# Transposes of the second query tile and one low value product given out first in each attention group

## The chip, the cores and the metric

The kernel runs on one core of one Trainium2 chip. The metric is the device time of one execution in microseconds (us); lower is better. A core has five engines, each with its own in-order instruction queue: PE (matrix products, its weight loads shown apart as PEld), DVE (vector), ACT (scalar functions, copies), POOL (vector work without access to PSUM) and SP, which here issues most of the memory transfers. PSUM is the accumulator memory that PE writes; DVE and ACT read it.

## The reference

One decoder layer on 2048 tokens of width 1024, in float32. The part that matters here is attention: 8 "forgetting" heads (softmax with a cumulative forget bias) and 8 "stick-breaking" heads, each of width 64, causal, then a product with the values.

```python
def one_block(args):                                  # forgetting heads, a block of 128 queries
    s = jnp.einsum('bhqd,bhkd->bhqk', q_blk, k) * scale
    s = s + F_blk[..., None] - F[:, :, None, :]
    s = jnp.where(causal, s, -jnp.inf)
    p = jax.nn.softmax(s, axis=-1)
    return jnp.einsum('bhqk,bhkd->bhqd', p, v)

def one_block(args):                                  # stick-breaking heads
    z = jnp.einsum('bhqd,bhkd->bhqk', q_blk, k) * scale
    log_one_minus_beta = jnp.where(strict, jax.nn.log_sigmoid(-z), 0.0)
    rest = lax.cumsum(log_one_minus_beta, axis=3, reverse=True) - log_one_minus_beta
    a = jnp.where(strict, jnp.exp(jax.nn.log_sigmoid(z) + rest), 0.0)
    return jnp.einsum('bhqk,bhkd->bhqd', a, v)
```

Around it stand a modulated RMS norm, one input projection (queries, keys, values, forget logits), a per-head norm, an output projection with a gated residual, and a gated MLP with a width-3 convolution. All of that is the same before and after.

## The kernel before, in words

The program runs in stages. First come the conditioning vector and the first 512 tokens' projections. Then come 32 attention units (stick-breaking heads first, then forgetting heads; four head pairs of each kind, and four blocks of 512 tokens for each pair). While a unit's attention runs, the projections of later units are issued between its pieces as filler: `L342` (queries and keys) and `L413` (values), whose inputs `hp` SP loads from memory at L468. Behind the last unit the output projection (L912), the MLP up (L1315) and the MLP down (L1614, L1609) follow.

Precision is kept by splitting each float32 operand into a high part, rounded to the faster type, and a low part, the rest. A product then needs several passes: high by high, high by low, low by high.

Inside a unit two query tiles of 128 rows are handled together (`qi` 0 and 1, the first and the second tile). For each tile `logits` (L596 and L597) puts a chunk of up to 512 logits into a PSUM bank `ps_qk` (two of them). For stick-breaking heads ACT makes two sigmoids `r` and `a` (L630, L631), POOL masks the diagonal (L633), and a DVE scan (L636) turns `a` into weights; `a` and `r` have seven buffers each. For forgetting heads DVE adds the bias and finds the row's extreme (L675), and ACT takes the exponential (L679) over the whole row.

Then `weighted` is called for each attention group, a pair of key blocks of 128 and two query tiles; there are 576 groups. It

- transposes up to four 128x128 blocks of weights on PE into one PSUM bank `ps_pt` (L606; three such banks): first those of the first query tile for key blocks 1 and 0, then those of the second tile for key blocks 0 and 1. In a group on the diagonal the first of the four is left out,
- copies the bank on ACT into the high half of the tile `at` (L610) and lets DVE subtract that copy from the bank into the low half (L611). `at` has three buffers,
- adds four products to the unit's accumulator `ps_pv` (L615): key block 0 by the high half, key block 0 by the low half, and the same for key block 1.

The order of instructions on each engine isn't the order of the code. A planner replays the program against its own model of times when the program is built, and puts into each engine's queue whatever is ready there first; ties go by the order of the code. So the two transposes of the first tile may be queued as soon as that tile's scan is done in the model, other work may come between them and the second tile's, and the high product may stand ahead of its low one with other work between. `tc.issue_after(x)` tells the planner that the instructions inside the block are to be queued behind `x` on the same engine. Each engine then runs its queue in order, and waits at an instruction whose inputs are not there.

When a head is done, ACT and DVE empty the accumulator (L737, L738). `ps_pv` has one buffer, so the next head's first product waits for that. At the end of a unit SP stores the result `oT` (L740), and SP's queue too is in order, so loads of `hp` behind that store wait with it.

## Time and profile before

| | |
|---|---|
| median of 3 runs | 2949.18 us (2945.81 to 2950.16) |
| the profiled execution: span from its first to its last instruction | 2941.4 us |
| busy share of PE / PEld / DVE / ACT / POOL | 97% / 84% / 74% / 57% / 31% |
| from 60 to 1440 us (attention with projections): PE busy | 1334.3 of 1380 us |
| in the same stretch: transposes L606, value products L615 | 2045 and 2158 PE instructions |

The page of the profile gives for its execution the span alone, no separate time with what lies around it. The span is 7.8 us (0.26%) under the median of the runs.

How to read it: a row of the timeline joins equal instructions that follow each other ("x4"), with the start of the first and the time from there to the end of the last. PE's instructions overlap: the next one starts long before the row's last one has ended, so what an instruction costs is the distance from one start to the next, not its duration. Ends on PE are modelled. "Idle before" is time in which the engine had nothing running before an instruction, with what ended it. The view of one line adds up such idle time on PE and on PEld for the same instruction, the view of waits gives the two apart.

### The profile page before, as it was taken

What the parts mean: (1) busy time and instruction counts of PE and PEld (TensorE: products, weight loads), DVE (VectorE), ACT (ScalarE), POOL (GpSimd) and SP (SyncE); (2) the same over time, 40 slices, a digit from 0 to 9 for tenths busy, and PEclk for the clock granted to TensorE, in tenths of its full rate; (3) what the DMA queues carried; (4) which work ended last, traced back from release to release, by engine and by line L of the source; (5) the groups of instructions that cost most, each with busy time, mean ns of one, the idle gap of its engine ahead of it and who ended that gap; (6) DMA issues with size and microseconds to landing.
All of it is one profiled execution on the core that took longest, in us unless ns stands there. A gap on an engine that the chain in (4) does not pass through costs nothing.

```text
span 2941.4 us, 45922 instructions
## 1 busy us (share of the span) xinstructions
PE 2867.8 (97%) x15772; PEld 2459.7 (84%) x15772; DVE 2179.5 (74%) x3464; ACT 1686.0 (57%) x3187; POOL 901.1 (31%) x967
## 2 busy tenths in 40 slices
PE   8999999999999999999999999999999999999998
PEld 7888888888988988888888788888788888888887
DVE  5787778877886656658843788888998888575476
ACT  5776767677776656658744554444444445433342
POOL 0431322243032423231213344444254543142200
PEclk8999999999999999999999999999999999999999
DMA  9749756867469794794537775554754444975644
GB/s 293 255 139 321 236 188 207 301 211 229 162 212 356 269 277 139 232 323 140 182 120 233 245 232 128 130 136 129 236 132 125 130 130 132 309 257 185 216 158 151
DMA packets 348346, 601.89 MB, mean 205 GB/s; under 512 B 34672, under 2 KB 178800, under 8 KB 348112
## 3 DMA queue, kind: packets, MB, share of 16 engines
q1 hardware_dynamic: 324208, 558.06, 57.7%
q0 software_dynamic: 10880, 20.97, 4.3%
q10 hardware_dynamic: 13024, 19.93, 1.9%
q8 instruction: 124, 2.03, 0.3%
q14 instruction: 110, 0.90, 0.1%
HBM read 420.77 MB, written 177.02 MB: 203 GB/s over the span
## 4 chain that ended last, share of the span: by engine, by line
PE 46%; DMA 3%; DVE 2%; SPq 1%; ACT 1%; issue 1%; POOL 0%; DVEq 0%; ACTq 0%; POOLq 0%
PE ps_o L1315 19%; PE ps_t L1315 7%; PE ps_o L1614 6%; PE ps_t L1614 3%; PE ps_bc L1614 3%; PE ps_o L912 1%; PE ps_pv L615 1%; DMA r<-rstd 1%; PE ps_bc L912 1%; PE ps_pt L606 1%; PE ps_o L1609 1%; DMA wo<-wos 1%; DMA hm<-hf_m 1%; SPq L895 1%; DVE op L46 1%
## 5 line engine op out<-in xcount | busy, mean ns | idle before, releaser
L1315 PE MATMUL ps_o<-op,wu 128*128 128x512 f32 x2592 | 608.0, 389 | 2.0 <-DVE snap L1366 1.5
L1315 PEld LDWEIGHTS ps_o<-op,wu 128*128 128x128 f32 x2592 | 486.2, 188 | 103.9 <-DVE snap L1366 1.9
L611 DVE TENSOR_TENSOR at<-ps_pt,at 128x512 fp32r<-128x512 f32 (+1 forms) x576 | 366.1, 652 | 100.2 <-ACT at L610 97.3
L636 DVE TENSOR_TENSOR_SCAN a<-r,a 128x512 f32<-128x512 f32 (+2 forms) x320 | 368.3, 1167 | 77.8 <-ACT a L631 39.9
L342 PE MATMUL ps_pj<-hp,w_qk 128*128 128x512 f32 x1512 | 411.2, 403 | 14.5 <-DMA hp<-hs 12.9
L610 ACT ACTIVATE at<-ps_pt 128x512 fp32r<-128x512 f32 (+1 forms) x576 | 318.5, 576 | 139.1 <-PE ps_pt L606 123.1
L615 PE MATMUL ps_pv<-at,V 128*128 128x256 f32 x2216 | 386.8, 292 | 9.3 <-DVE at L611 4.2
L615 PEld LDWEIGHTS ps_pv<-at,V 128*128 128x128 f32 x2216 | 320.9, 190 | 39.8 <-DVE at L611 11.4
L342 PEld LDWEIGHTS ps_pj<-hp,w_qk 128*128 128x128 f32 x1512 | 275.4, 190 | 71.0 <-DMA hp<-hs 16.2
L45 ACT ACTIVATE wu<-wuraw 128x512 fp32r<-128x512 f32 x204 | 128.9, 632 | 248.5 <-PE ps_o L1315 190.1
L596 PE MATMUL ps_qk<-K,Q 128*128 128x512 f32 (+2 forms) x640 | 265.7, 416 | 5.6 <-ACT a L631 3.3
L413 PE MATMUL ps_pj<-w_v,hp 128*128 128x256 f32 (+1 forms) x1536 | 236.6, 288 | 2.1 <-DVE hp L422 1.6
L597 PE MATMUL ps_qk<-K,Q 128*128 128x512 f32 (+2 forms) x640 | 235.7, 369 | 0.0
L1315 PE MATMUL ps_t<-op,wu 128*128 128x512 f32 x888 | 220.8, 390 | 1.0 <-DVE op L46 1.0
L413 PEld LDWEIGHTS ps_pj<-w_v,hp 128*128 128x128 f32 x1536 | 209.0, 189 | 10.9 <-DVE q L373 1.5
L630 ACT ACTIVATE r<-ps_qk 128x512 f32<-128x512 f32 (+2 forms) x320 | 173.1, 541 | 58.2 <-PE ps_qk L597 55.5
L46 DVE TENSOR_TENSOR wu<-wuraw,wu 128x512 fp32r<-128x512 f32 x204 | 189.6, 930 | 18.1 <-ACT wu L45 16.7
L1315 PEld LDWEIGHTS ps_t<-op,wu 128*128 128x128 f32 x888 | 166.4, 188 | 36.5 <-DVE op L46 1.8
L606 PE MATMUL ps_pt<-edge,a 128*128 128x128 f32 x1088 | 185.1, 274 | 8.4 <-DVE a L636 7.8
L1614 PE MATMUL ps_o<-op 128*128 128x512 f32 x840 | 191.5, 389 | 0.0
L1614 PEld LDWEIGHTS ps_o<-op 128*128 128x128 f32 x840 | 157.7, 188 | 32.7
L679 ACT ACTIVATE p<-p,mn 128x128 f32<-128x128 f32 (+15 forms) x128 | 153.9, 1203 | 53.3 <-DVE mn L675 52.2
(342 smaller groups left out, 5237.6 us busy)
## 6 DMA issues: line engine op xcount, KB each, us to landing
hp<-hs SPq DMA_DIRECT2D x224, 512.0 KB
wuraw<-in_w_up_dram SPq DMA_DIRECT2D x80, 512.0 KB
ra<-g SPq DMA_DIRECT2D x136, 256.0 KB
rb<-in_w_down_dram SPq DMA_DIRECT2D x108, 256.0 KB
g<-u SPq DMA_DIRECT2D x80, 256.0 KB
hs<-hp SPq DMA_DIRECT2D x32, 512.0 KB
hp<-in_w_ada_dram SPq DMA_DIRECT2D x32, 512.0 KB
qk_fox<-q SPq DMA_DIRECT2D x32, 512.0 KB
```

The source lines that it names most:

```text
L46: (lo_engine or nc.gpsimd).tensor_sub(lo, src, f(hi))
L342: nc.tensor.matmul(acc, w[kt][:, a, n], h[:, bb], start=kt == 0 and i == 0, stop=kt == KT - 1 and i == 2)
L413: nc.tensor.matmul(av[:, t * width:(t + 1) * width], hts[kt][:, a, tok], w[1][kt][:, bb, 0:width], start=kt == 0 and m == 0, stop=kt == KT ...
L596: nc.tensor.matmul(b[:, :cw], Q[:, hl, 0, qcols], K[:, hl, :cw], start=True, stop=False)
L597: marks.append(nc.tensor.matmul(b[:, :cw], Q[:, hl, 1, qcols], K[:, hl, :cw], start=False, stop=True).ins)
L606: nc.tensor.transpose(b[:, i * P:(i + 1) * P], blk(kts[kk], qi), ident)
L610: copies = [nc.scalar.activation(at[:, 0, lo:], b[:, lo:], AF.Copy).ins, nc.vector.tensor_sub(at[:, 1, lo:], b[:, lo:], f(at[:, 0, lo:])).ins]
L611: nc.vector.tensor_sub(at[:, 1, lo:], b[:, lo:], f(at[:, 0, lo:])).ins]
L615: m = nc.tensor.matmul(o[:, 0:2 * P], V[kt // 4][:, kt % 4, hl, :], rhs, start=first and kk == 0 and w == 0, stop=last and kk == 1 and w == 1)
L636: nc.vector.tensor_tensor_scan(rev, r[:, 0:need][:, ::-1], rev, 0.0 if right[qi] is None else right[qi][:, 0:1], ALU.mult, ALU.add)
L1315: nc.tensor.matmul(b, w[:, p, j], o[:, q], start=first and i == 0, stop=last and i == 2, skip_group_check=True)
L1614: nc.tensor.matmul(b, a[:, p, t * P:(t + 1) * P], w[:, q], start=first and i == 0, stop=last and i == 2, skip_group_check=True)
```

## The change

Inside `weighted` the order of the transposes in the code is turned round: second tile, key block 1, then second tile, key block 0, then the first tile's two. The first one given out becomes `lead`, and the other three are to be queued behind it. Of the products the low one of each key block now stands ahead of the high one, and the first high product is to be queued behind the first low one. The same instructions run on the same data; the accumulator's start and stop flags move with the order.

```diff
         order = [(1, 0), (0, 0), (0, 1), (1, 1)]
-        for i, (kk, qi) in enumerate(order):
+        lead = None
+        for i in (3, 2, 1, 0):
+            kk, qi = order[i]
             if not (diag and i == 0):
-                nc.tensor.transpose(b[:, i * P:(i + 1) * P], blk(kts[kk], qi), ident)
+                with tc.issue_after(lead) if lead else nullcontext():
+                    m = nc.tensor.transpose(b[:, i * P:(i + 1) * P], blk(kts[kk], qi), ident).ins
+                lead = lead or m
...
         for kk, kt in enumerate(kts):
-            for w in range(2):
+            for w in (1, 0):
                 rhs = at[:, w].rearrange("p (s q) -> p s q", q=P)[:, 0:4:3, :] if kk else at[:, w, P:3 * P]
-                m = nc.tensor.matmul(o[:, 0:2 * P], V[kt // 4][:, kt % 4, hl, :], rhs,
-                                     start=first and kk == 0 and w == 0, stop=last and kk == 1 and w == 1)
+                with tc.issue_after(lead) if kk == 0 and w == 0 else nullcontext():
+                    m = nc.tensor.matmul(o[:, 0:2 * P], V[kt // 4][:, kt % 4, hl, :], rhs,
+                                         start=first and kk == 0 and w == 1, stop=last and kk == 1 and w == 0)
+                lead = m.ins
```

Six lines are added in all, so L606 and L615 of before are L609 and L620 of the change, and all lines behind are six further on.

The planner makes another queue of it. Two places on PE in the middle of the stick-breaking units follow. `a` are weights of one query tile (10119 the first and 10127 the second tile of one chunk, 10163 and 10171 of the next), `ps_pt` a transpose bank, `at` the copied group; L596 and L597 are logits, L413 and L342 filler. The transposes of two groups, before:

```order
L606 MATMUL ps_pt_10131<-edge_249,a_10119 128x128 x2
L413 MATMUL ps_pj_10320<-w_v_8431,hp_9906 128x256 x2
L413 MATMUL ps_pj_10320<-w_v_8436,hp_9911 128x256 x2
L606 MATMUL ps_pt_10147<-edge_249,a_10119 128x128 x2
L596 MATMUL ps_qk_10167<-K_8603,Q_9362 128x512
L597 MATMUL ps_qk_10167<-K_8603,Q_9362 128x512
L413 MATMUL ps_pj_10320<-w_v_8436,hp_9911 128x256
L413 MATMUL ps_pj_10320<-w_v_8441,hp_9948 128x256 x3
L413 MATMUL ps_pj_10320<-w_v_8446,hp_9953 128x256 x2
L606 MATMUL ps_pt_10131<-edge_249,a_10127 128x128 x2
L606 MATMUL ps_pt_10147<-edge_249,a_10127 128x128 x2
```

The same two groups with the change:

```order
L596 MATMUL ps_qk_10167<-K_8603,Q_9362 128x512
L597 MATMUL ps_qk_10167<-K_8603,Q_9362 128x512
L413 MATMUL ps_pj_10320<-w_v_8446,hp_9953 128x256 x3
L413 MATMUL ps_pj_10320<-w_v_8451,hp_9970 128x256 x3
L609 MATMUL ps_pt_10131<-edge_249,a_10127 128x128 x2
L609 MATMUL ps_pt_10131<-edge_249,a_10119 128x128 x2
L609 MATMUL ps_pt_10147<-edge_249,a_10127 128x128 x2
L609 MATMUL ps_pt_10147<-edge_249,a_10119 128x128 x2
```

The first tile's transposes moved behind the second tile's; the logits and the filler that stood between them stand ahead of all, and each bank is filled at one go.

The value products of the same groups on PE a little later, before:

```order
L342 MATMUL ps_pj_10502<-hp_10503,w_qk_8381 128x512 x3
L615 MATMUL ps_pv_10057<-at_10132,V_8838 128x256
L606 MATMUL ps_pt_10188<-edge_249,a_10171 128x128 x2
L615 MATMUL ps_pv_10057<-at_10132,V_8838 128x256 x3
L615 MATMUL ps_pv_10057<-at_10148,V_8838 128x256
L606 MATMUL ps_pt_10212<-edge_249,a_10163 128x128 x2
L606 MATMUL ps_pt_10212<-edge_249,a_10171 128x128 x2
L342 MATMUL ps_pj_10502<-hp_10508,w_qk_8386 128x512 x3
L615 MATMUL ps_pv_10057<-at_10148,V_8838 128x256 x3
```

And with the change:

```order
L342 MATMUL ps_pj_10502<-hp_10503,w_qk_8381 128x512 x3
L609 MATMUL ps_pt_10188<-edge_249,a_10171 128x128 x2
L609 MATMUL ps_pt_10188<-edge_249,a_10163 128x128 x2
L620 MATMUL ps_pv_10057<-at_10132,V_8838 128x256 x4
L609 MATMUL ps_pt_10212<-edge_249,a_10171 128x128 x2
L609 MATMUL ps_pt_10212<-edge_249,a_10163 128x128 x2
L342 MATMUL ps_pj_10502<-hp_10508,w_qk_8386 128x512 x3
L620 MATMUL ps_pv_10057<-at_10148,V_8838 128x256 x4
```

Before, one high product went ahead and three followed behind other work. With the change a group's four products stand together, at the place where the three stood.

Over the whole program the two orders hold the same instructions on every engine. The queue of PE has 687 unbroken runs of the groups' transposes before and 485 now, and 662 unbroken runs of value products before and 482 now. On ACT, DVE, POOL and SP some instructions change places with neighbours inside the attention stage; behind it every queue is as it was.

## Prediction

> **What bounds the kernel now.** I read the busy shares and the granted clock first, then busy time by stage, then the waits on PE, then single places in time.
>
> ```profile
> PE 2867.8 (97%) x15772; PEld 2459.7 (84%) x15772; DVE 2179.5 (74%) x3464; ACT 1686.0 (57%) x3187; POOL 901.1 (31%) x967
> PEclk8999999999999999999999999999999999999999
> 60.00:1440.00 1380.00, 1334.29 (x8803) 1190.25 (x8802) 1030.48 (x1860) 970.97 (x2011) 399.19 (x512) 0.99 0.71 234
> 1440.00:2941.00 1501.00, 1481.94 (x6717) 1225.15 (x6715) 1112.68 (x1514) 681.91 (x1108) 501.24 (x450) 1.00 0.57 173
> ```
>
> The reader is to see that PE sets the end: it is busy for 97% of the span at a granted clock of 0.99 to 1.00 nearly throughout, so no other engine's saving counts unless PE waits for it. The window rows give PE, PEld, DVE, ACT and POOL in this order. The change touches the first window alone. There PE is without work for 1380 - 1334 = 46 us. Those 46 us, and whatever PE pays for going to and fro between kinds of work, are all that a new order can win; the same products remain.
>
> What PE waits for in that window, in total, times, longest:
>
> ```profile
> PE ps_pj L342 <- DMA hp<-hs: 12.9, 8, 6.0
> PE ps_pt L606 <- DVE a L636: 7.8, 16, 1.5
> PE ps_pv L615 <- DVE at L611: 4.2, 9, 1.0
> PE ps_qk L596 <- ACT a L631: 3.3, 6, 1.1
> PE ps_pv L615 <- DVE oT L738: 2.6, 4, 1.3
> PE ps_pv L615 <- ACT at L610: 1.6, 3, 0.6
> ```
>
> So three of the six largest waits are at instructions that the change moves: transposes that wait for the scan, and value products that wait for DVE's or ACT's half of `at`. The largest one, filler that waits for `hp`, isn't touched directly.
>
> **Fewer changes of work on PE.** The queue has 202 fewer runs of transposes and 180 fewer of value products (687 to 485 and 662 to 482, counted in the two orders). What does one run cost beside its instructions? Starts on PE, from the timeline:
>
> ```profile
> 798.84 0.38 PE L606 MATMUL ps_pt<-edge,a 128*128 128x128 f32 x2
> 798.98 0.72 PE L413 MATMUL ps_pj<-w_v,hp 128*128 128x256 f32 x4
> 799.54 0.38 PE L606 MATMUL ps_pt<-edge,a 128*128 128x128 f32 x2
> ...
> 800.23 0.87 PE L413 MATMUL ps_pj<-w_v,hp 128*128 128x256 f32 x6
> 800.94 0.60 PE L606 MATMUL ps_pt<-edge,a 128*128 128x128 f32 x4
> ...
> 1413.14 1.47 PE L606 MATMUL ps_pt<-edge,p 128*128 128x128 f32 x12
> 1414.37 0.48 PE L596 MATMUL ps_qk<-K,Q 128*128 128x512 f32 x1
> 1414.68 0.40 PE L597 MATMUL ps_qk<-K,Q 128*128 128x512 f32 x1
> 1414.91 0.40 PE L596 MATMUL ps_qk<-K,Q 128*128 128x512 f32 x1
> ```
>
> Six filler products take 800.94 - 800.23 = 0.71 us, 0.118 each. From 798.84 to 799.54 lie two transposes and four such products: 0.70 - 0.47 = 0.23 us for the two. The run of twelve and one logits product take 1414.68 - 1413.14 = 1.54; the product's pitch is 1414.91 - 1414.68 = 0.23, so twelve transposes take 1.31, 0.109 each. Two would take 0.218 in a long run and take 0.227 alone: about 0.01 us for the run itself. 202 runs by 0.01 are 2 us. The rows are rounded to 0.01, so the bounds are 0 and 4. Runs of value products cost nothing extra: the lone one below starts 0.12 us before what follows it, the pitch of any product of its size.
>
> **Waits of the value products.** The second place shown with the change, as it ran before:
>
> ```profile
> 803.89 0.86 PE L342 MATMUL ps_pj<-hp,w_qk 128*128 128x512 f32 x3
> 804.58 0.28 PE L615 MATMUL ps_pv<-at,V 128*128 128x256 f32 x1
> 804.70 0.38 PE L606 MATMUL ps_pt<-edge,a 128*128 128x128 f32 x2
> 805.20 0.74 PE L615 MATMUL ps_pv<-at,V 128*128 128x256 f32 x4
> ```
>
> The high product goes at 804.58, two transposes follow, and then the low product holds the queue: the two transposes need 0.23, yet the next start is 0.50 behind theirs. Both halves have a duration:
>
> ```profile
> L610 ACT ACTIVATE at<-ps_pt x540: 462/597/719, 80.4 to 1436.9; 128x512 fp32r<-128x512 f32 x134, 128x384 fp32r<-128x384 f32 x46
> L611 DVE TENSOR_TENSOR at<-ps_pt,at x540: 495/680/694, 84.6 to 1438.8; 128x512 fp32r<-128x512 f32 x134, 128x384 fp32r<-128x384 f32 x46
> L606 PE MATMUL ps_pt<-edge,a x1088: 270/272/421, 74.7 to 868.0; 128*128 128x128 f32 x182
> ```
>
> With the medians a group's high half is there 0.27 + 0.60 = 0.87 us after its last transpose starts, and the low half 0.68 later, at 1.55, if neither engine has a queue. I added up the pitches (0.109, 0.118, 0.23) along both queues. The low product stands on average 4.6 us behind its group's transposes before and now; under 2.0 us in 29 of 576 groups before, in 36 now, and the missing time up to 2.0 sums to 10.8 us before and 12.4 now. The high product stood under 1.3 us behind in 13 groups (3.4 us missing); with the change it has the low one ahead of it, so it never waits. What these waits cost, with PEld's idle time counted in:
>
> ```profile
>   DVE at L611: 16.2, 37
>   ACT at L610: 7.7, 14
>   DVE oT L738: 6.8, 10
> ```
>
> The wait for ACT, 7.7 us, is what can go. The wait for `oT` stays, since the head's first product has it whichever half it is. The wait for DVE stays and may grow by 12.4 - 10.8 = 1.6. The bounds are 7.7 won and 1.6 lost. I take 3 won, near the 3.4 that the queue shows missing, because PE that doesn't stop at the high product reaches the low one sooner, and part of the time returns there.
>
> The high product stood on average 4.1 us behind the transposes, so it goes 0.5 us later now; nothing waits for it alone, since the accumulator is read behind all four.
>
> **Waits of the transposes.** The idle time before L606, with PEld's, has two rows that matter:
>
> ```profile
>   DVE a L636: 17.4, 30
>   DVE at L611: 2.9, 7
> ```
>
> The first is the scan being late, the second a bank not yet free. A group had two places to stop, at the first and at the second tile; now the one ahead is the later. Along the queues, the first tile's transposes stand on average 5.5 us behind its logits before and 6.9 now; the second tile's 5.5 and 5.7. So the first tile's stops go: at most half of 17.4, 8.7 us. They don't all stay away, because a scan that is late for the first tile makes the second tile's late as well: the two follow each other on DVE. I take a third, 3 us; the bounds are 0 and 8.7. A bank is held between its first and its last transpose for 1.25 us before and 0.46 now, on average, which bears on the 2.9 us; I take nothing for it and keep 0 to 2.9.
>
> **The sum.** 2 + 3 + 3 = 8 us less. The profiled execution's span of 2941.4 becomes 2933; the runs' median lies 7.8 above that span, so 2949.2 becomes 2941. All the upper bounds together, 4 + 7.7 + 8.7 + 2.9, make 23 us and 2926; the lower bounds make 1.6 us lost, 2951. ACT, DVE, POOL and SP have the same instructions and run beside PE, so nothing is added for them where they aren't waited for.
>
> **The rivals.**
>
> *The waits only change place.* DVE's scans and subtractions are the same and come in the same order, so if PE in these places only waits for DVE to come along, each microsecond saved at the first stop is spent at the second. For it speaks that low products wait 37 times against 14 for the high, and that both can wait in one group:
>
> ```profile
> 655.06 0.38 PE L615 MATMUL ps_pv<-at,V 128*128 128x256 f32 x1 [0.62 <-ACT at L610]
> 655.78 0.62 PE L615 MATMUL ps_pv<-at,V 128*128 128x256 f32 x3 [0.34 <-DVE at L611]
> ```
>
> Here the high product waits for ACT, and the low ones behind it for DVE. Against it: a first tile's scan that is late by chance needn't make the second late. Then only the run's price remains: 2949.2 - 2 = 2947.
>
> *Waits of first tiles and high products go wholly*, and banks are free earlier: 2926, the sum of the bounds. For it: the low product's cover is no shorter on average. Against it is the pairing above.
>
> *The low product holds up the queue.* The product with the later input now stands in front of the one with the earlier input, and all behind it stands still, as the row at 805.20 shows. If each of the 36 groups with under 2.0 us of cover pays DVE's 0.68 for it once more, 24 us are lost and 2 won: 2949.2 + 22 = 2971. Against it: the same low products stood in the queue before, and the missing time grows by 1.6 us, not by 24.
>
> [...]
>
> *SP's queue runs later, and filler waits for `hp`.* This is the case on the other side.
>
> ```profile
> SPq L740 <- DVE oT L738: 65.5, 16, 12.4
> ```
>
> At a unit's end the store of `oT` waits at the head of SP's queue, 16 times for up to 12.4 us, and the loads of `hp` behind it wait too; then L342 stops for 12.9 us in 8 waits. With the change a head's last high product can't go ahead of its low one, and the planner places the loads afresh. If as many loads again come too late, 13 us are lost and 2 won: 2949.2 + 11 = 2960. It decides from the point where a load's lead is used up; most loads have one, since filler waits only 8 times. Against it, the last value product of a group is where it was, behind DVE.
>
> That the change doesn't do what it says is excluded by the order: all groups' four products stand together.
>
> **How the numbers follow.** The forecast, part of the waits gone, has a chance of 0.47, within 2931 to 2947. That waits only move has 0.27, that they go wholly 0.10, that the low product holds up the queue 0.03, that loads come late 0.13. A measurement of this kernel can tell about 0.2% from no change, so faster is below 2943.3 and slower above 2955.1. Faster takes three quarters of the forecast, 0.36, all of the third case, 0.10, and the part of the second where runs save their 4 us and a little more, 0.05: 0.51. Slower takes the two cases of loss, 0.16, and 0.02 of the others: 0.18. Between lies 0.31. The range for 8 in 10 goes from 2926, the sum of the bounds, to 2958, inside the late loads.
>
> **What would show it right or wrong.** In the changed kernel's waits, value products waiting for ACT should be near nothing; those waiting for DVE within a few us of before. Transposes should wait for the scan less, below 12 us in the view of their line. A lone value product in the timeline should be gone. If the wait for DVE grows by what the wait for ACT loses, waits only move. If L342's wait for `hp` goes past 20 us, the late loads decide, and if PE's time behind 1440 us changed, the whole picture would be wrong, because nothing there moved.

## The result and the profile after

| | before | with the change |
|---|---|---|
| median of the runs on one chip | 2948.89 us (6 runs, 2945.81 to 2953.7) | 2964.95 us (6 runs, 2961.95 to 2970.71) |
| span of the profiled execution | 2941.4 us | 2963.9 us |

The change costs 0.6%: the ratio is 1.006, with a 95% interval of 1.0049 to 1.0071. The forecast was 2941 us within 2926 to 2958, so the time moved the other way than forecast and lies outside the range.

The busy shares and the granted clock of the changed kernel, and the window of attention (columns: length of the window, then busy time of PE, PEld, DVE, ACT and POOL with the number of instructions, granted clock, DMA share, GB/s):

```profile
PE 2875.8 (97%) x15772; PEld 2468.9 (83%) x15772; DVE 2175.8 (73%) x3464; ACT 1683.7 (57%) x3187; POOL 894.0 (30%) x967
PEclk8999999999999999999999999999999999999999
60.00:1440.00 1380.00, 1324.66 (x8717) 1185.29 (x8716) 1016.33 (x1831) 956.27 (x1989) 386.53 (x503) 0.99 0.70 232
```

The number of instructions is the same on every engine. In the attention window PE is without work for 55 us, where it was 46, and it gets through 8717 instructions there, not 8803. Nothing happens behind attention: the 2592 products of the first kind in the MLP up take the same 826 us, only 22.6 us later. The line's own view, before and after (shortest, median and longest duration in ns, then first and last start in us):

```profile
L1315 PE MATMUL ps_o<-op,wu x2592: 387/389/501, 1686.9 to 2513.4; 128*128 128x512 f32 x200
```

```profile
L1321 PE MATMUL ps_o<-op,wu x2592: 387/389/497, 1709.5 to 2535.8; 128*128 128x512 f32 x200
```

What PE waits for with the change, over the whole execution (in total, times, longest; with the change the copy and the subtraction of `at` are L614 and L615; the rows of before that the prediction shows read the same in that view):

```profile
PE ps_pj L342 <- DMA hp<-hs: 14.2, 10, 4.8
PE ps_pv L620 <- DVE at L615: 7.8, 9, 2.0
PE ps_qk L596 <- ACT a L637: 7.6, 9, 3.4
PE ps_pt L609 <- DVE a L642: 6.8, 11, 2.1
PE ps_pt L609 <- DVE at L615: 3.7, 2, 2.2
PE ps_pv L620 <- DVE oT L744: 3.6, 5, 1.8
```

Value products wait for ACT no more, as forecast, and the filler's wait for `hp` is about what it was (12.9 before). What stands out is the last column. The longest wait of a value product for DVE was 1.0 and is 2.0, that of logits for a free bank was 1.1 and is 3.4, that of transposes for the scan was 1.5 and is 2.1.

**Where the time goes.** I took all starts on PE from 60 us to the last value product, subtracted the pitch of the instruction ahead (0.23 us for 512 columns, 0.17 for 384, 0.118 for 256, 0.109 for a transpose), and sorted what is left over by size. The last value product starts at 1514.1 us before and at 1532.1 now, 18.0 later:

| left over between two starts | before | with the change | difference |
|---|---|---|---|
| over 1.5 us each | 15.9 us in 5 places | 31.1 us in 13 places | +15.2 |
| 0.25 to 1.5 us each | 47.5 us in 83 places | 46.0 us in 82 places | -1.5 |
| under 0.25 us each | 49.0 us | 53.2 us | +4.2 |

So the many middling waits, on which the prediction's sums were made, changed by 1.5 us in all. The loss is in a few long stops. One of the 13 (at 1462.1 us) stands just at the limit of 1.5. The sums of the two lower rows depend on how the pitches are rounded, by some us in the last; their differences change by less than 1 us. Filler that waits for `hp` makes 9.7 us of the long stops before (2 places) and 10.1 now (3); the growth is in the other places, 3 before and 10 now. The remaining 4.9 us come between the last value product and the first product of the MLP up (156.8 us before, 161.7 now).

One such stop with the change, on PE and on ACT:

```profile
495.90 0.72 PE L620 MATMUL ps_pv<-at,V 128*128 128x256 f32 x4
500.04 0.39 PE L596 MATMUL ps_qk<-K,Q 128*128 128x256 f32 x1 [3.42 <-ACT a L637]
```

```profile
498.51 1.15 ACT L45 ACTIVATE q<-xt 128x512 fp32r<-128x512 f32 x2 [5.58 <-DMA Q<-qk_sb]
499.57 0.26 ACT L636 ACTIVATE r<-ps_qk 128x128 f32<-128x128 f32 x1
499.72 0.27 ACT L637 ACTIVATE a<-ps_qk 128x128 f32<-128x128 f32 x1
```

PE waits for the sigmoids, which free a bank of logits. The sigmoids could run, but in ACT's queue two copies of `q` for a later unit stand ahead of them, and ACT stands idle for 5.58 us. Their input `xt` is made by POOL, which starts on it at 496.13 us, after 20.13 us of waiting for a transfer. Another, on DVE:

```profile
863.76 0.49 PE L609 MATMUL ps_pt<-edge,a 128*128 128x128 f32 x3
866.41 0.79 PE L609 MATMUL ps_pt<-edge,a 128*128 128x128 f32 x4 [2.17 <-DVE at L615]
```

```profile
864.35 1.41 DVE L755 SCALAR_TENSOR_TENSOR hp<-hp,cols 128x512 f32<-128x512 f32 x2 [1.25 <-DMA hp<-in_w_out_dram]
865.68 0.68 DVE L615 TENSOR_TENSOR at<-ps_pt,at 128x512 fp32r<-128x512 f32 x1
```

Here the scaling of the output projection's weights waits for its load, and the subtraction behind it holds the bank that the transposes need.

**The clock.** With the change, PE's granted clock is half in eight stretches of the attention stage, and six of them begin 0.4 to 2.0 us behind a stop of 1.5 us or more. The stop at 866.41 and what follows, in windows of the changed kernel (the clock is the third number from the end):

```profile
863.90:866.30 2.40, 0.35 (x4) 0.11 (x1) 1.96 (x4) 2.38 (x7) 0.29 (x1) 1.00 0.99 317
866.80:870.20 3.40, 3.40 (x15) 3.11 (x14) 3.40 (x5) 2.68 (x6) 3.19 (x2) 0.50 0.94 302
870.30:874.00 3.70, 3.70 (x25) 3.28 (x24) 3.70 (x5) 2.17 (x4) 0.62 (x1) 1.00 1.04 373
```

PE stood for about 2.2 us and then worked for 3.4 us at a granted clock of 0.50, which by that share loses another 1.7, an estimate. In the attention stretch the time at half clock was 17.1 us in the profiled execution of before and is 30.7 now. An execution of the same order of before, shown below among the experiments, has 30.7 too, so this part isn't shown to be the change's doing. By the granted 0.50, 13.6 us more at half clock lose about 6.8, an estimate, which would account for the two profiles lying 22.5 us apart and the medians 16. A run's time lies some 1.7 us above its own span (2965.58 and 2963.9 for the change), so the profile of before, with a span of 2941.4, shows an execution faster than each of the six timed ones.

### The profile page after: what moved, and what is told of

It reads as the page before. It is cut to its first block, busy times and chain, and to the rows that moved or that the text cites. A ratio compares the mean times of both kernels' runs of the same rounds, so it can differ in the third digit from the quotient of the medians.

```text
span 2963.9 us, 45907 instructions
## 1 busy us (share of the span) xinstructions
PE 2875.8 (97%) x15772; PEld 2468.9 (83%) x15772; DVE 2175.8 (73%) x3464; ACT 1683.7 (57%) x3187; POOL 894.0 (30%) x967
## 4 chain that ended last, share of the span: by engine, by line
PE 77%; DMA 12%; DVE 4%; ACT 3%; issue 2%; POOL 2%; SPq 1%; ACTq 0%; POOLq 0%; DVEq 0%
PE ps_o L1321 19%; PE ps_pj L342 8%; PE ps_t L1321 7%; PE ps_pv L620 7%; PE ps_o L1620 6%; PE ps_pt L609 5%; PE ps_pj L413 5%; PE ps_t L1620 3%; PE ps_qk L596 3%; PE ps_bc L1620 3%; PE ps_qk L597 3%; PE ps_o L918 3%; DMA hp<-hs 2%; DMA hp<-in_w_ada_dram 1%; DMA vd<-xt 1%
## 5 line engine op out<-in xcount | busy, mean ns | idle before, releaser
L615 DVE TENSOR_TENSOR at<-ps_pt,at 128x512 fp32r<-128x512 f32 (+1 forms) x576 | 366.6, 652 | 114.4 <-ACT at L614 111.7
L342 PE MATMUL ps_pj<-hp,w_qk 128*128 128x512 f32 x1512 | 407.9, 402 | 17.3 <-DMA hp<-hs 14.2
L642 DVE TENSOR_TENSOR_SCAN a<-r,a 128x512 f32<-128x512 f32 (+2 forms) x320 | 363.7, 1155 | 78.8 <-POOL a L639 37.8
L614 ACT ACTIVATE at<-ps_pt 128x512 fp32r<-128x512 f32 (+1 forms) x576 | 320.5, 577 | 165.4 <-PE ps_pt L609 136.0
L620 PE MATMUL ps_pv<-at,V 128*128 128x256 f32 x2216 | 357.6, 291 | 12.1 <-DVE at L615 7.8
L620 PEld LDWEIGHTS ps_pv<-at,V 128*128 128x128 f32 x2216 | 310.6, 191 | 38.0 <-DVE at L615 15.8
L342 PEld LDWEIGHTS ps_pj<-hp,w_qk 128*128 128x128 f32 x1512 | 277.6, 190 | 77.1 <-DMA hp<-hs 18.2
L596 PE MATMUL ps_qk<-K,Q 128*128 128x512 f32 (+2 forms) x640 | 258.6, 405 | 12.8 <-ACT a L637 7.6
L597 PE MATMUL ps_qk<-K,Q 128*128 128x512 f32 (+2 forms) x640 | 235.3, 369 | 0.0
L413 PE MATMUL ps_pj<-w_v,hp 128*128 128x256 f32 (+1 forms) x1536 | 228.8, 287 | 1.6 <-DVE hp L422 1.6
L413 PEld LDWEIGHTS ps_pj<-w_v,hp 128*128 128x128 f32 x1536 | 207.0, 189 | 10.7 <-PE ps_pv L620 1.1
L636 ACT ACTIVATE r<-ps_qk 128x512 f32<-128x512 f32 (+2 forms) x320 | 172.9, 540 | 43.9 <-PE ps_qk L597 42.3
L609 PE MATMUL ps_pt<-edge,a 128*128 128x128 f32 x1088 | 167.1, 276 | 10.2 <-DVE a L642 6.8
```

What stands on the lines that cost most here:

```text
L342: nc.tensor.matmul(acc, w[kt][:, a, n], h[:, bb], start=kt == 0 and i == 0, stop=kt == KT - 1 and i == 2)
L413: nc.tensor.matmul(av[:, t * width:(t + 1) * width], hts[kt][:, a, tok], w[1][kt][:, bb, 0:width], start=kt == 0 and m == 0, stop=kt == KT ...
L596: nc.tensor.matmul(b[:, :cw], Q[:, hl, 0, qcols], K[:, hl, :cw], start=True, stop=False)
L597: marks.append(nc.tensor.matmul(b[:, :cw], Q[:, hl, 1, qcols], K[:, hl, :cw], start=False, stop=True).ins)
L609: m = nc.tensor.transpose(b[:, i * P:(i + 1) * P], blk(kts[kk], qi), ident).ins
L614: copies = [nc.scalar.activation(at[:, 0, lo:], b[:, lo:], AF.Copy).ins, nc.vector.tensor_sub(at[:, 1, lo:], b[:, lo:], f(at[:, 0, lo:])).ins]
```

## The experiments

In most of them the order on an engine is held: behind the program's instructions an ordering edge without a semaphore is added from each instruction of an engine to the next in a given list, so the planner can't place them anew. All ratios are to the kernel before, on the same chip, with 95% intervals; they are worked out from all runs and need not be the ratio of the two medians.

```diff
+def _freeze(nc, tc):                    # the lists: the queues as they stood in one of the two kernels
+    for chain in orders:
+        for a, b in zip(chain, chain[1:]):
+            tc.add_manual_dep(ins[b], ins[a].name, no_sync, reason="queue order")
...
     tile_trunk_kernel(tc, *args)
+    _freeze(nc, tc)
```

### Which queue carries the loss

The change with ACT, DVE, POOL and SP held in the order of before, PE planned anew:

> The change as it is, but the queues of ACT, DVE, POOL and SP hold exactly the instructions' order of before (a chain of order-only edges through each of these four queues); PE alone is ordered anew, with 476 runs of transposes and 489 of value products (before 687 and 662, the change 485 and 482). Theory A, the grouping itself costs (PE has less loose work to put into a wait): the time stays near the change's, 2960 to 2970 us, and the granted clock stays near 0.989. Theory B, the other engines' queues were planned worse and PE only pays for it: it falls back to before or a little under, 2940 to 2951 us, with a clock of 0.993.

The code of before with those four queues in the order that the change gives them, PE planned anew:

> Before's code, with the split transposes and products, but the queues of ACT, DVE, POOL and SP in the order that they have with the change; PE is ordered anew (683 runs of transposes, 671 of value products). Theory A: near before, 2943 to 2953 us. Theory B: near the change, 2958 to 2970 us, with PE stops of 1.5 us and more where ACT's queue holds logits work behind a copy that waits for a load, and a clock of 0.989.

Measured: 2964.91 us, ratio 1.0059 (1.0036 to 1.0081), and 2973.05 us, 1.0075 (1.005 to 1.0101). Both are slow. Theory A fits the first run and misses the second; theory B misses the first and has the side of the second, which is slower than its range. The first has the old order on four engines, and the loss stays; the second has no grouping at all, and the loss is there. So neither the new order of the four queues nor the grouping is needed for it. What the two have in common is that PE was planned anew.

### The two halves of the change

Only the transposes (the second hunk of the diff left out), and only the products:

```diff
-        for i, (kk, qi) in enumerate(order):
+        for i in (3, 2, 1, 0):          # with lead, as in the change; products as before
```

> Only the transposes of the change (second tile first, the others behind it), the products as before; all queues planned anew. If the transposes carry the loss (theory A with the first tile's weights held longer): 2957 to 2970 us. If the products carry it: 2943 to 2953. Theory B gives no sign: any new plan may land between 2945 and 2970.

```diff
-            for w in range(2):
+            for w in (1, 0):            # with lead, as in the change; transposes as before
```

> Only the products of the change (low part first, high behind it), the transposes as before; all queues planned anew. If the products carry the loss (theory A with the low product holding up the queue): 2957 to 2970 us. If the transposes carry it: 2943 to 2953. Theory B gives no sign: any new plan may land between 2945 and 2970.

Measured: 2962.62 us, 1.0048 (1.0029 to 1.0067), and 2957.67 us, 1.0028 (1.0011 to 1.0046). Each half costs something when the planner places all work anew. Each is a new plan of its own; their sum, 0.76%, can't be told from the whole's 0.6% with these intervals.

### The grouping alone, with nothing else moved

All five queues are held as before, but on PE 284 split groups' transposes stand together at the second tile's place, and each group's four products, low half first, at the first low one's place:

```diff
-orders["PE"] = before
+orders["PE"] = grouped(before)          # 454 runs of transposes and 453 of products; other queues as before
```

> All five queues stand exactly as before (order-only edges through each of them), except inside the groups: in 284 of the 298 groups whose transposes were split, the first tile's transposes move down to the second tile's, and in all 576 groups the four products stand together, low part first, where the first low one stood. 454 runs of transposes and 453 of value products (before 687 and 662). Nothing is planned anew. Theory A, the grouping itself costs: 2957 to 2970 us. Theory C, any newly made plan loses against the one before, and the grouping by itself costs nothing: 2940 to 2952 us, by the terms of the prediction 2941.

The same with the transposes alone (products as before):

> As the last one, with only the transposes moved (284 groups), the products as before; 458 runs of transposes, 620 of value products. Theory A with the transposes as its cause: 2955 to 2965 us. Theory A with the products as its cause, and theory C: 2942 to 2952 us.

And the control, the kernel before with all queues held just as they are:

> The kernel before, with every engine's queue held in exactly the order that it has. Every theory expects the time of before, within 0.15%; what it differs by is what holding the queues costs in itself, which bears on the two kernels with grouped work in held queues (2951 and 2953 us).

Measured: 2950.98 us, 1.0012 (0.9999 to 1.0025); 2953.47 us, 1.0009 (0.9997 to 1.0021); the control 2947.51 us, 1.0001 (0.9987 to 1.0015). Holding the queues costs nothing that can be told, and grouping by itself does neither good nor harm that can be told. The 8 us of the forecast (0.27%) are outside its interval. The slow kernel at 2964.91 has the same four queues as the grouped one at 2950.98, and both group; they differ in where the groups and the filler stand on PE. So there it was PE's new order around the groups that cost some 0.47% (the ratios 1.0059 and 1.0012, on two chips).

The profile shows why the grouping wins nothing. PE's and PEld's idle time ahead of value products and of transposes between 60 and 1440 us, in the held kernel before (above the dots L615, below them L606):

```profile
  DVE at L611: 13.5, 34
  ACT at L610: 9.5, 14
  DVE oT L738: 7.4, 9
...
  DVE a L636: 17.1, 29
  ACT p L679: 4.9, 8
  PE ps_qk L597: 2.2, 4
```

The same two views of the grouped kernel, where the rows on ACT at L610 and on ps_qk are gone:

```profile
  DVE at L611: 29.7, 49
  DVE oT L738: 10.4, 12
...
  DVE a L636: 14.1, 23
  ACT p L679: 1.8, 4
```

The wait for ACT, 9.5 us, is gone; the wait for DVE at the same place has grown by 16.2. Transposes gain 8.3 us in these three rows, value products lose 9.7. The waits have changed place. With the transposes alone grouped, value products wait 11.8 us for DVE and 5.4 for ACT, so the growth comes with the products grouped, low half first.

### Other plans of the same two programs

If any new plan is a draw, a small setting that has nothing to do with the grouping should move the time as much. Three settings, each with the old rule and with the change's: the delay of a head's variance sum, the lag between making weights and using them, and the pace at which filler is due.

```diff
-            deferred.append([reduce, 13])
+            deferred.append([reduce, 12])
...
-    LAG, ENDQ = 12, 16
+    LAG, ENDQ = 13, 16
...
-                  min(1.0, m / (0.8 * n))
+                  min(1.0, m / (0.85 * n))
```

> Before's code with one number changed that has nothing to do with the groups: the small products of the head variance are given out 12 instead of 13 steps after a unit's half (252 of 15553 products on PE, the same work). All queues are planned anew. Theory C: slower by 5 to 20 us than before, 2954 to 2970, with a granted clock under 0.992, as any new plan. Theory A: within 4 us of before, 2945 to 2953.

> The change, and with it the number of the head variance's products at 12 instead of 13 (the same step with before's code cost 28 us, 2977). Theory C, a new plan is a new draw and the grouping costs nothing by itself: anywhere between 2945 and 2980, not tied to 2965 nor to 2977. Theory A, the grouping costs 16 us on any plan: above its partner, 2985 to 3000.

> Before's code with another such number: filler is tied to the logits of 13 instead of 12 pieces back. All queues are planned anew; the groups' rule is the one of before. Theory C: 2954 to 2970 us. Theory A: 2945 to 2953.

> The change, with the filler's lag at 13 instead of 12 (with before's code 2950 us). Theory C: between 2945 and 2980. Theory A: 16 us above its partner, 2960 to 2972.

> Before's code with the projections' pace within a unit at 0.85 instead of 0.8; nothing in the groups changes. Theory C: a new draw, 2947 to 2977. Theory A: within 4 us of before, 2945 to 2953.

> The change with the pace at 0.85: the partner of the run before it. Theory C: a new draw, 2945 to 2980, above or under its partner. Theory A: 16 us above its partner.

| setting | old rule: us, ratio (interval) | the change's rule: us, ratio (interval) |
|---|---|---|
| as it is | (the kernel before) | 2964.95, 1.006 (1.0049 to 1.0071) |
| variance sum 12 | 2976.94, 1.0097 (1.0074 to 1.012) | 2955.85, 1.0016 (0.9999 to 1.0033) |
| lag 13 | 2950.04, 1.001 (0.9995 to 1.0025) | 2956.38, 1.0018 (1.0002 to 1.0034) |
| pace 0.85 | 2953.53, 1.0018 (1.0 to 1.0036) | 2976.41, 1.0091 (1.0071 to 1.0112) |

Putting off a sum by one step less costs 1% with the old rule, more than the change does, and with that setting the change's rule is the faster one by 0.8%. In the three pairs the change's rule lies 0.81% under, 0.08% over and 0.73% over its partner, so a fixed cost of the grouping (theory A) isn't seen. Theory C's own ranges missed twice: 2977 lies over its 2970, and 2950 under its 2954. The old rule lies between 0 and 0.97%, the change's between 0.16 and 0.91%. None of the other seven plans beats the kernel before, nor do the two made from one half of the change; two of the seven can't be told from it, and two more only just. The means, 0.31% and 0.46%, are too close for four draws each to tell a cost of the rule from none.

### Is it a handful of copies?

The timeline names the offenders, so they can be moved. All queues are held as the change has them; seven instructions go later in their queues, past the attention's work that waits behind them.

```diff
-orders = after
+orders = after                          # ACT: w_qk copy (315.5 us) by 2 places, two q copies (498.5 us) by 4
+                                        # DVE: four scalings of hp (864.3 and 928.4 us) by 5
```

> The changed kernel, with every engine's queue held in exactly the order that it has (the control for the two repairs). Every theory expects the change's time, 2961 to 2969 us, some 0.5% above the kernel before, with PE's long stops where they were: at 316.7, 319.1, 395.3, 500.0, 866.4 and 930.4 us among others.

> The changed kernel with every queue held as it is, but seven instructions go later: on ACT the copy of w_qk at 315.5 us by two places and the two copies of q from xt at 498.5 us by four, on DVE the four scalings of hp at 864.3 and 928.4 us by five. Nothing else moves. If background copies with late loads ahead of the attention's work make the stops, those at 316.7 and 319.1 (1.8 and 1.9 us), 500.0 (3.6), 866.4 (2.3) and 930.4 (1.8) shrink below 1 us each, and three stretches of half the granted clock behind them (1.7 us lost in each) stay away: 8 to 16 us less than the held control, 2949 to 2957. If the stops are only where a shortage shows that lies elsewhere (the grouping itself, or the loads' rate), they come back a little later and the time is the control's within 3 us, 2962 to 2968.

> As the kernel with seven instructions moved, but only the three on ACT. By the late copies, the stops at 316.7, 319.1 and 500.0 go and two stretches of half clock with them: 5 to 10 us less than the held control, 2954 to 2961; those at 866.4 and 930.4 stay. By the rival, the control's time within 3 us.

Measured: the control 2964.27 us, 1.0052 (1.0036 to 1.0068); all seven moved 2966.49 us, 1.0064 (1.0046 to 1.0082); three on ACT moved 2966.44 us, 1.0062 (1.0044 to 1.0079). Nothing is won: the theory that moving this handful of copies brings the time back falls. The timeline of the kernel with all seven moved shows where the stops went, on PE and on ACT:

```profile
502.65 0.63 PE L620 MATMUL ps_pv<-at,V 128*128 128x256 f32 x4
506.94 0.44 PE L596 MATMUL ps_qk<-K,Q 128*128 128x384 f32 x1 [3.65 <-ACT a L637]
```

```profile
505.34 0.42 ACT L45 ACTIVATE w_qk<-raw_qk 128x256 fp32r<-128x256 f32 x1 [4.09 <-DMA raw_qk<-in_w_in_dram]
505.66 0.58 ACT L614 ACTIVATE at<-ps_pt 128x512 fp32r<-128x512 f32 x1
```

The copies of `q` are out of the way, and the next background copy in ACT's queue, one of `w_qk`, waits 4.09 us for its own load. That would fit a whole run of background work that stands too early against its loads, but no run tests it. There are 13 long stops in the control and 13 here (34.6 and 34.8 us). Two of the latter, 5.3 us together, lie at 69.9 and 166.6 us, ahead of the first instruction that was moved, where both kernels have the same queues; so much can differ between two executions.

The two held controls also make the cleanest pair: the order of before and that of the change, profiled at 2948.1 and 2963.4 us. Long stops are 18.6 us in 8 places and 34.6 us in 13; middling waits 43.5 and 43.9 us; half clock within attention 30.7 us in both. The long stops differ by 16.0 us, the spans by 15.3. Of these 16.0, 7.0 are at filler that waits for `hp` (2 places before, 4 with the change). The row of that wait, first before, then with the change:

```profile
PE ps_pj L342 <- DMA hp<-hs: 7.9, 5, 3.5
```

```profile
PE ps_pj L342 <- DMA hp<-hs: 16.7, 9, 5.7
```

It grew by 8.8 us here and by 1.3 between the first two profiles (12.9 and 14.2), while two executions of the order of before differ by 5.0 in it. How much of it is the plan's can't be told from single profiles.

### Is it SP's queue?

If the loads come late because SP gives them out later, SP's old order should help. All else is held as changed:

```diff
-orders["SP"] = after["SP"]
+orders["SP"] = before["SP"]             # 299 of 1779 places differ; second kernel: POOL too (174 of 1092)
```

> The changed kernel with PE, ACT, DVE and POOL held in the order that the change gives them, and SP's queue held in the order that it had before. If loads that the new plan gives out later on SP's queue make the added stops (the prediction's rival of the late loads), most of them go: 8 to 16 us less than the held change, 2949 to 2957. If SP's order only follows the others, the time is that of the held change within 3 us, 2961 to 2967.

> As the kernel with SP's queue as before, and POOL's queue as before too; PE, ACT and DVE stay in the order that the change gives them. If the loss sits in the order on PE, ACT and DVE together, 2961 to 2967, as the held change; if SP and POOL carry it, 2949 to 2957.

Measured: 2973.16 us, 1.0079 (1.0061 to 1.0096), and 2980.47 us, 1.0117 (1.0102 to 1.0132). Neither theory had this: putting queues back makes it worse, by 0.3% and then by another 0.4%. What PE waits for most with SP and POOL put back:

```profile
PE ps_pj L342 <- DMA hp<-hs: 17.7, 8, 5.6
PE ps_pt L609 <- DVE a L642: 15.7, 11, 4.2
...
PE ps_pt L722 <- DVE at L615: 4.7, 1, 4.7
```

The rows have longest waits of 4 to 6 us. SP's order in the change fits the other queues of the change; putting the old one back doesn't take the loss away. These runs speak for how the queues stand to each other, and not for one queue.

### All runs together

I counted the long stops (over 1.5 us, by starts on PE as above) in all 20 profiled executions: two of before and after, 18 of the experiments. Their sum lies between 15.9 us (before) and 47.3 us (SP and POOL put back), and the span between 2941.4 and 2985.8. The correlation of the two is 0.90, and each microsecond of long stops goes with 1.35 us of span. The middling waits (0.25 to 1.5 us) lie between 37.8 and 50.5 us and have a correlation of 0.25. The time at half clock in the attention stretch has 0.81, and goes with the long stops (0.79), so the two can't be parted. On the whole, then, the long stops tell a slow plan from a fast one, though not each one: with 24.5 us of them lag 13 of the old rule has a span of 2948.5, and with 26.0 us the change with four old queues has 2962.8. This is a relation over 20 executions and no proof of a cause; moving seven instructions away from the stops didn't lower the time.

## Why the prediction was wrong, point by point

**What bounds the kernel: right.** PE at 97%, its idle time in the attention window, nothing behind attention that changes by itself. The list of waits leaves out its fourth row, `PE ps_pt L564 <- DVE xm L567: 3.9, 3, 2.8`, so of the six largest waits two, not three, are at instructions that the change moves and can shorten; the sum doesn't use this count.

**Fewer changes of work on PE, 2 us: not seen.** With 454 and 453 runs, fewer than the change has, and nothing else moved, the time is 0.12% above before with an interval from -0.01 to 0.25%. If the 2 us were won, they were paid back elsewhere; the run can't tell these apart.

**Waits of the value products, 3 us won: wrong in the sum.** The wait for ACT went wholly, the upper bound of 7.7. But the wait for DVE was to grow by 1.6 us at most. It grew from 16.2 to 22.7 us in the change, by 6.5, in the same view that the prediction quoted:

```profile
  DVE at L615: 22.7, 38
  DVE oT L744: 9.2, 13
```

With all else held it grew by 16.2, while the 9.5 for ACT went. The step that failed is the bound of 1.6, the cover counted from pitches along the queues: it took each low product's missing time as if PE ran without any other stop. The prediction did say that PE reaches the low product sooner when it doesn't stop at the high one, and let 4.7 of 7.7 us return for it; more than all of it returned. Why more than all isn't shown.

**Waits of the transposes, 3 us won: the size came out, the choice of rows didn't.** With all else held the wait for the scan fell from 17.1 to 14.1, 3.0 us. That is partly luck: two executions of the same order of before give 16.2 and 13.5 for value products' wait for DVE, so a figure of 3 us is no larger than what a single profile can be off by. The prediction also said that two rows matter and passed over two that are larger than its second, ACT p L679 (4.3) and PE ps_qk L597 (3.4); with all else held these gave 5.3 of the 8.3 us. In the change the wait for the scan fell to 10.5, but the wait for a bank, for which I took no cost, rose from 2.9 to 8.3:

```profile
  DVE a L642: 10.5, 18
  DVE at L615: 8.3, 5
```

One of those five is the stop at 866.41, behind a scaling that waits for its load.

**The sum: this is what failed.** It failed twice. The first failure is the edit's own gain: forecast at 8 us, it didn't come when the edit was made with all else held (2950.98 us, 0.12% above before), since the waits of the value products came back at DVE as told above. The second and larger one is a term that isn't there, the new plan. The sum counts the places that the edit names and takes everything else as it was; its last sentence says it for the other engines: "ACT, DVE, POOL and SP have the same instructions and run beside PE, so nothing is added for them where they aren't waited for." The front of this document said that instructions change places on those engines, and its first place shows that logits and filler moved on PE as well. From the grouping in the old plan (0.12%) to the change (0.6%) the new plan costs some 0.48%, about 14 us. With the other four queues held as before, a new plan of PE alone cost as much (0.47%).

How a new plan costs time is shown in single places only. At some of the stops above, a background copy or scaling whose load is still under way comes ahead of attention's work, ACT or DVE stands still, and then PE. In the views of waits on ACT between 60 and 1530 us such idle time is, before and after:

```profile
ACT hp L782 <- DMA hp<-in_w_ada_dram: 23.5, 17, 4.9
...
ACT w_v L45 <- DMA raw_v<-in_w_in_dram: 1.4, 1, 1.4
```

```profile
ACT hp L788 <- DMA hp<-in_w_ada_dram: 30.9, 15, 4.5
...
ACT q L45 <- DMA Q<-qk_sb: 5.6, 1, 5.6
...
ACT w_v L45 <- DMA raw_v<-in_w_in_dram: 4.0, 7, 1.2
```

All rows of that kind sum to 38.9 us before and 54.4 after. But this isn't the whole cause, and it isn't needed for the loss: the change with four old queues is as slow with 42.5 us, and before's code with the new ones slower still with 44.0, while the held order of before has 40.5. Of the change's 13 long stops, four (at 316.7, 395.3, 500.0 and 866.4 us, 10.0 us together) have such a wait of over 1 us on ACT or DVE right ahead of them. Missing, then, was a term for the new plan by its measured spread: 0.1 to 0.97% (3 to 28 us) in the nine new plans measured here, the smallest of them not clear of no change, and none of them a gain.

**The rivals.** *The waits only change place* (0.27) is what the grouping by itself does: 2947 was said, 2951 measured with all else held, and the profile has it row by row. It should have been the forecast for the edit itself. *SP's queue runs later, and filler waits for `hp`* (0.13, 2960) had the side and about the size, and late loads as the cause. But by its own test, a wait of L342 past 20 us, it didn't happen: 14.2. In the pair with held queues the same wait did grow, from 7.9 to 16.7, still under its mark; so the rival isn't settled as a part of the cause. As the whole it falls: with the four old queues the loss is there and that wait is 9.7, and SP's old order makes it worse. *The low product holds up the queue* (0.03, 2971) was right that all behind a waiting product stands still (at 805.20 of before the next start is 0.50 us behind two transposes that need 0.23); its price of 24 us was to fall on many short waits, and the middling ones didn't grow in sum.

**What was to show it.** A wait for ACT near nothing: yes. The scan below 12 us in the view of the line: yes, 10.5. No lone value product: yes. These three came out as said and the kernel was slower, since they test the edit's places and not the plan. Two more signs were named. The wait for DVE was to stay within a few us of before, and grew by 6.5 in the view of the line. And if it grew by what the wait for ACT loses, waits only move: it did nearly that (7.7 lost, 6.5 grown), so by the prediction's own sign the first rival was the right one for these places.

**What stays open.** Why this plan has 13 long stops and the old one 5 to 8 isn't settled. It isn't the grouping by itself, and putting off seven instructions or putting back SP's and POOL's order doesn't mend it. A new plan of PE is enough for a loss of that size with the old order on the other four; which part of it does it isn't known, nor what the held orders of PE, ACT and DVE each carry in the change itself, since none of these three was put back alone. The kernel before is the fastest of ten plans; the runs don't show what makes it so. If it had been picked as the fastest among many, any new plan would tend to be slower; that isn't on record either. Whether the grouping would cost something on the mean over many plans can't be told from four pairs.

## What to carry to other kernels

When a planner sets the order, an edit to a few lines is two changes, what the lines do and a new plan for everything else: price the second by the spread that unrelated small settings give (here 0 to 1%), and tell the two apart by holding all queues as they were and making the edit alone. A wait that is taken away at one instruction is to be looked for at the next one behind it in the same queue before it is counted as won (in the grouped kernel 9.5 us at ACT went and 16.2 at DVE came). Look for the loss in the longest wait of each row and not only in the totals, and follow a stop back through the queue of the engine that is waited for, to the work that stands ahead and the load that it waits for (at 500.04 us, two copies of `q` on ACT behind an idle time of 5.58 us).

## What the runs showed of the hardware

Six of the eight stretches at half clock follow long stops here. With the change, a window of the timeline with two stops of under 2 us, and the windows of the clock around it; the second set is from before at the same times, with no stop:

```profile
316.74 0.44 PE L596 MATMUL ps_qk<-K,Q 128*128 128x384 f32 x1 [1.67 <-ACT a L637]
317.02 0.34 PE L597 MATMUL ps_qk<-K,Q 128*128 128x384 f32 x1
319.11 0.74 PE L620 MATMUL ps_pv<-at,V 128*128 128x256 f32 x4 [1.76 <-DVE oT L744]
...
320.16 2.32 PE L342 MATMUL ps_pj<-hp,w_qk 128*128 128x512 f32 x6
```

```profile
318.80:320.60 1.80, 1.49 (x8) 1.33 (x9) 1.39 (x3) 1.54 (x5) 1.11 (x3) 1.00 1.03 410
320.70:324.10 3.40, 3.40 (x15) 3.02 (x13) 3.17 (x4) 1.74 (x5) 2.66 (x3) 0.50 1.03 411
324.20:328.00 3.80, 3.80 (x24) 3.30 (x24) 2.58 (x5) 3.00 (x8) 0.29 (x1) 1.00 1.04 358
```

```profile
320.70:324.10 3.40, 3.40 (x24) 2.95 (x23) 3.26 (x5) 3.35 (x11) 2.16 (x5) 1.00 1.07 405
```

In these 3.4 us PE runs 15 products and transposes; at the same times before, with another mix of them, it runs 24. In the stretch behind 866.41 eight value products take 1.71 us, 0.214 each, where their pitch at a clock of 1.00 is 0.118. In the attention stretch the time at half clock comes in pieces of 3.41 and 6.83 us: one and two of them before, seven and one with the change.

Of these eight with the change, six begin 0.4 to 2.0 us behind the stops at 319.1, 395.3, 500.0, 660.9, 866.4 and 1462.1 us (1.5 to 3.6 us each, by starts as above; ahead of the first of them stands the one at 316.7, 1.8 us). One begins at 1215.0, inside a stop of 4.9 us, and one at 156.8 follows stops of 0.6 and 1.2 us alone. Not every long stop has one: none follows those at 92.2, 930.4, 1059.5, 1165.2 and 1415.8 us, of 1.7 to 3.3 us. What decides it isn't shown here.

Two remarks on the engines, in numbers of the profile before. Products of operands left in plain float32 are slower: of the two at 777.44 us (L790, 128x512, 592 ns each, 1.02 us together) the second starts 0.43 us behind the first, where the pitch of products of rounded operands is 0.23 at that size. And none of POOL's 967 instructions has a PSUM tile among its operands; whether it could reach one isn't shown.
